# A sliding-window copy made of DMAs alone: twelve staged batches for eleven, and direct copies issued as halves

## The chip, the cores and the metric

The kernel runs on one core of one Trainium2 chip. Nothing is computed: every byte is moved by the core's 16 DMA engines, which serve three DMA queues, one issued from SyncE (SP, queue q1 in the profile), one from ScalarE (ACT, queue q10) and one from GpSimd (POOL, queue q0, a queue whose transfers software prepares). The metric is the device time of one execution in microseconds, the median of several runs.

## The reference: what is computed

```python
batch, length, dim = (32, 4096, 256)     # x is float32
window_size, stride = 64, 32
n_windows = (length - window_size) // stride + 1        # 127
for i in range(n_windows):
    start = i * stride
    result[:, i] = x[:, start:start + window_size].copy()
```

Since the window is two strides long, it is easiest to think in blocks of 32 rows, 32 KB each. A batch has 128 blocks, and window w of a batch is block w followed by block w + 1, 64 KB in one piece. So the output is nearly twice the input: 32 x 127 windows of 64 KB, 266 MB, from 134 MB.

## The kernel before

There are two ways to make a batch, and the kernel uses both at once.

**Direct.** `Copier.windows` (lines 29 to 38) copies from HBM to HBM. One call takes 16 windows, a "sixteen", so that each of the 16 engines gets one window. With `half=None` the call copies whole windows, 64 KB for each engine, 1 MB in all; the profile shows a window as two packets of 32 KB. With `half=0` or `1` it copies only the first or second block of each of the 16 windows, 32 KB for each engine and 512 KB in all, so that a sixteen takes two calls. A direct byte passes the DMA engines once, and is read from HBM as often as it is written.

**Staged.** `Staging.load` and `Staging.store` (lines 86 to 111) bring a batch into one of six SBUF tiles, a block to each of the 128 partitions, and store that tile twice: once as the first halves of all windows (`half=0`) and once as the second halves (`half=1`). A staged byte passes the engines once on its way in and twice on its way out, but is read from HBM once. The packets have 16 KB. `Staging.run` (line 116) issues all this on ScalarE's queue in the order six loads, twelve stores, then the loads and stores of the second group; a load waits until its tile's earlier stores are done.

A whole-tile store writes 128 half windows where a batch has 127, so it spills one junk half window into the batch before and one into the batch after. The neighbours are direct batches, and the 15 windows next to a staged batch are therefore kept out of the sixteens. These are the "edges" (lines 166 to 168): 20 of them with 15 windows, and one with 4. GpSimd's queue copies them at the end, after waiting for the neighbour's stores (`st.wait_stored`, line 196).

**Which batches.** Before, `staged` (line 143) is 1, 4, 7, ..., 31, eleven batches; the other 21 are direct, with seven sixteens each, 147 in all, every direct batch having one staged neighbour. Batch 31 is shifted by one block so that its spill falls into batch 30, whose last windows are copied by `columns` (lines 40 to 47), which cuts windows into 4 KB pieces; the very last two windows are issued from SyncE after batch 31's stores (lines 202 and 203).

**The order on SyncE.** The loop of line 175 issues the sixteens. A hand-made account (`turns`, `share`, lines 170 to 187) chooses between whole and halves: three sixteens in four are halved while ScalarE's queue loads, and 15 in 100 while it stores, with all halves at the start and near the second group of loads. In all 92 sixteens go whole and 55 as halves.

**The release of the software queue.** The semaphore `near` is raised by the last but one sixteen. GpSimd waits for it on line 192 and then issues its edges, the order being that of the list. The kernel ends when SyncE has seen all the counts (line 206).

Of the kernel before, what the change touches and what calls it, by code (L numbers as in the profile page):

```python
# [125 lines left out]
@with_exitstack  # L126
def kernel(
    ctx: ExitStack,
    tc: tile.TileContext,
    x: bass.AP,  # L130
    window_size: bass.AP,
    stride: bass.AP,
    out: bass.AP,
):
    nc = tc.nc
    W, S = int(window_size), int(stride)
    B, L, D = x.shape
    n_win = (L - W) // S + 1
    assert out.shape == (B, n_win, W, D)
    c = Copier(x, out, B, L, D, W, S, n_win)  # L140


    staged = [*range(1, B, 3)]
    items = [(b, -1 if b == B - 1 else 0, c.nb) for b in staged]
    place = {b: g for g, (b, _, n) in enumerate(items) if n == c.nb}
    direct = [b for b in range(B) if b not in staged]
    pool = ctx.enter_context(tc.tile_pool(name="xb", bufs=1))
    st = Staging(c, tc, pool, x.dtype, items, 6)
    ring_d, ring_s, ring_r = nc.sync, nc.scalar, nc.gpsimd
    done = tc.alloc_semaphore("done")  # L150
    near = tc.alloc_semaphore("near")
    rest = tc.alloc_semaphore("rest")
    total = {done: 0, near: 0, rest: 0}

    def count(dma, sem):
        dma.then_inc(sem, 16)
        total[sem] += 16

    sixteens = []
    for b in direct:
        w = 15 if b - 1 in staged else 0
        sixteens += [(b, w + 16 * j) for j in range((c.nw - w) // 16)]
    singles = [(B - 1, c.nw - 1, 1)]
    edges = [(b, 0 if b - 1 in staged else 112, 15) for b in direct[:-1]]
    last = B - 2
    edges.append((last, 112, 4))

    first_loads, loads, stores = 6 * 17, 5 * 17, 6 * 34  # L170
    turns = share = 0
    with tc.tile_critical():  # L172
        st.run(ring_s)

        for i, (b, w) in enumerate(sixteens):
            sem = near if i == len(sixteens) - 2 else done
            second = turns - first_loads - stores
            loading = turns < first_loads or 0 <= second < loads
            share += 120 if turns < 16 or -8 <= second < 16 else 90 if loading else 18
            if share >= 120:  # L180
                share -= 120
                turns += 4
                count(c.windows(ring_d, b, w, 16, 0), done)
                count(c.windows(ring_d, b, w, 16, 1), sem)
            else:
                turns += 3
                count(c.windows(ring_d, b, w, 16), sem)
            if i == len(sixteens) // 2:
                for b, w, half in singles:
                    count(c.windows(ring_d, b, w, 1, half, 2048), done)  # L190

        ring_r.wait_ge(near, 16)
        for b, w, n in edges:
            for k in (b - 1, b + 1):
                if k in place and b != last:
                    st.wait_stored(ring_r, place[k])
            count(c.windows(ring_r, b, w, n), rest)


        count(c.columns(ring_r, last, 116, 9), rest)  # L200
        ring_r.drain()  # L201
        st.wait_stored(ring_d, place[B - 1])
        count(c.columns(ring_d, last, 125, 2), done)
        total[st.ended] = st.count[st.ended]
        for sem, n in total.items():
            ring_d.wait_ge(sem, n)
# [35 lines left out]
```

## Time and profile before

| what | value |
|---|---|
| device time, median of 3 runs | 754.17 us (752.58 to 754.21) |
| span of the profiled execution | 742.1 us |
| median less the span (launch and end around the span) | 12.1 us |
| bytes that the DMA engines moved | 313.26 MB |
| HBM bytes read, written | 220.95 MB, 267.09 MB |
| SyncE: 1 MB copies, 512 KB copies | 92, 110 |
| ScalarE: loads, stores of 4 MB | 10, 21 (and ten smaller pieces) |
| GpSimd: edges of 960 KB | 20 |
| POOL's long wait for `near` | 648.7 us |

The profile gives the span of the execution that it recorded, and no device time of its own for it; what lies around the span is taken from the median, which makes the profiled execution's time 742.1 + 12.1 = 754.2 us. Packets are what the profile counts as a DMA engine's unit of work. Besides the data packets there is a completion packet of 4 bytes for each engine and DMA, which raises the semaphore. A DMA share of 1.00 means that all 16 engines are busy the whole time; it can come out slightly over 1, since the recorded times of following packets overlap a little.

### The profile page before, as it was taken

The page shows a single profiled execution, that of the slowest core. Times are in us where ns is not written, and L with a number is a line of the kernel's source. Part 1 is how long each engine was busy: PE and PEld are TensorE (multiplying, and loading weights), DVE is VectorE, ACT ScalarE, POOL GpSimd, SP SyncE. Part 2 cuts the span into 40 slices and gives each one's busy share as a digit, 9 for nine tenths or more (in the row PEclk, how much of TensorE's full clock was granted, in tenths as well). Part 3 has the DMA queues.
Part 4 walks back from the last instruction along what each step waited for, and adds up shares of the span by engine and source line. Part 5 has one row for each costly group of instructions (what it writes and reads, how often), then busy time and mean ns, then how long its engine had stood idle before and what let it go on. Part 6 is the DMA issues. An engine that isn't in the chain of part 4 may idle for free.

```text
span 742.1 us, 323 instructions
## 1 busy us (share of the span) xinstructions
POOL 12.7 (2%) x26
## 2 busy tenths in 40 slices
POOL 0000000000000000000000000000000000050100
DMA  8999999999999999999999999999999999999996
GB/s 361 424 430 427 435 431 428 423 435 425 428 427 426 428 428 420 429 435 427 427 427 412 433 435 431 427 436 432 434 424 429 430 424 426 428 435 432 421 420 253
DMA packets 18290, 313.26 MB, mean 422 GB/s; under 512 B 4336, under 2 KB 4336, under 8 KB 4528
## 3 DMA queue, kind: packets, MB, share of 16 engines
q1 hardware_dynamic: 8016, 154.32, 48.8%
q10 hardware_dynamic: 9104, 138.41, 44.0%
q0 software_dynamic: 1168, 20.51, 6.6%
q14 instruction: 2, 0.02, 0.0%
HBM read 220.95 MB, written 267.09 MB: 658 GB/s over the span
## 4 chain that ended last, share of the span: by engine, by line
another core or an unknown queue 92%; POOL 2%; issue 0%; POOLq 0%; SPq 0%
POOL out_dram L34 2%; POOLq L201 0%; POOLq L237 0%; SPq L172 0%; POOLq L114 0%
## 5 line engine op out<-in xcount | busy, mean ns | idle before, releaser
L34 POOL DMA_DIRECT2D out_dram<-in_x_dram x21 | 12.0, 575 | 685.4 <-DMA out_dram<-in_x_dram 648.7
L44 POOL DMA_DIRECT2D out_dram<-in_x_dram x1 | 0.6, 581 | 0.0
L223 POOL MEMSET const-float32-0.0<- 128x1 f32 x1 | 0.1, 98 | 0.2 <-issue 0.2
L223 POOL MEMSET const-bfloat16-1.0<- 128x1 bf16 x1 | 0.1, 101 | 0.0
L223 POOL MEMSET const-float32-1.0<- 128x1 f32 x1 | 0.1, 98 | 0.0
L223 POOL MEMSET const-uint8-127<- 128x1 uint8 x1 | 0.1, 98 | 0.0
## 6 DMA issues: line engine op xcount, KB each, us to landing
out_dram<-in_x_dram SPq DMA_DIRECT2D x92, 1024.0 KB, 99.8
out_dram<-xb ACTq DMA_DIRECT2D x21, 4096.0 KB, 138.5
out_dram<-in_x_dram SPq DMA_DIRECT2D x110, 512.0 KB, 90.2
xb<-in_x_dram ACTq DMA_DIRECT2D x10, 4096.0 KB, 130.5
out_dram<-in_x_dram POOLq DMA_DIRECT2D x20, 960.0 KB, 37.9
xb<-in_x_dram ACTq DMA_DIRECT2D x4, 1024.0 KB, 15.7
out_dram<-xb ACTq DMA_DIRECT2D x2, 1024.0 KB, 110.5
out_dram<-xb ACTq DMA_DIRECT2D x4, 512.0 KB, 94.4
```

The costliest lines, as they stand in the source:

```text
L34: return q.dma_start(out=self.oap((b * self.nw + w0) * 2 + h, [[2 * blk, n], row]), in_=self.xap(b * self.nb + w0 + h, [[blk, n], row]), m ...
L44: return q.dma_start(out=self.oap((b * self.nw + w0) * 2, [[part, 16], [2 * self.blk, n], row]), in_=self.xap(b * self.nb + w0, [[part, 16 ...
L223: nc = _bacc.Bacc("TRN2", target_bir_lowering=False, num_devices=1)
```

## The change

- Twelve batches are staged: 1, 4, 7, 10, 13, 16, 18, 20, 22, 25, 28 and 31. The 20 others are direct and have seven sixteens each, 140 in all. Batches 17, 19 and 21 now have a staged neighbour on both sides, so their sixteens begin at window 7, and they have two edges, of 7 and of 8 windows.
- The account of turns is gone. Every sixteen is issued as two halves, but for every eighth (the fifth, the thirteenth and so on), which goes whole: 17 whole, 123 as halves.
- Eight of the 16 edges that have 15 windows are issued as two halves each and stand in the list after the first four edges. The edge of batch 30 has 11 windows instead of 4, a number worked out so that the windows of all unsplit edges add up to a multiple of 16; the `columns` copy on GpSimd shrinks from 9 windows to 2.
- `near` is raised by the last but two sixteen.

```diff
-    staged = [*range(1, B, 3)]
+    staged = [1, 4, 7, 10, 13, 16, 18, 20, 22, 25, 28, B - 1]
...
-    sixteens = []
+    sixteens, edges, split = [], [], []
+    last = B - 2
     for b in direct:
-        w = 15 if b - 1 in staged else 0
-        sixteens += [(b, w + 16 * j) for j in range((c.nw - w) // 16)]
+        first = (15 if b + 1 not in staged else 7) if b - 1 in staged else 0
+        sixteens += [(b, first + 16 * j) for j in range((c.nw - first) // 16)]
+        if b != last:
+            edges += [(b, w, n, None) for w, n in ((0, first), (first + 112, 15 - first)) if n]
+    for e in [e for e in edges if e[2] == 15][4:12]:
+        edges.remove(e)
+        split += [e[:3] + (half,) for half in (0, 1)]
     singles = [(B - 1, c.nw - 1, 1)]
-    edges = [(b, 0 if b - 1 in staged else 112, 15) for b in direct[:-1]]
-    last = B - 2
-    edges.append((last, 112, 4))
-
-    first_loads, loads, stores = 6 * 17, 5 * 17, 6 * 34
-    turns = share = 0
+    odd = -sum(n for _, _, n, _ in edges) % 16
+    edges = edges[:4] + split + edges[4:] + [(last, 112, odd, None)]
+    whole = 8
+
     with tc.tile_critical():
         st.run(ring_s)
 
         for i, (b, w) in enumerate(sixteens):
-            sem = near if i == len(sixteens) - 2 else done
...
-            if share >= 120:
-                share -= 120
-                turns += 4
-                count(c.windows(ring_d, b, w, 16, 0), done)
-                count(c.windows(ring_d, b, w, 16, 1), sem)
-            else:
-                turns += 3
-                count(c.windows(ring_d, b, w, 16), sem)
+            for half in (None,) if i % whole == whole // 2 else (0, 1):
+                dma = c.windows(ring_d, b, w, 16, half)
+                count(dma, near if i == len(sixteens) - 3 and half != 0 else done)
...
-        for b, w, n in edges:
+        for b, w, n, half in edges:
             for k in (b - 1, b + 1):
                 if k in place and b != last:
                     st.wait_stored(ring_r, place[k])
-            count(c.windows(ring_r, b, w, n), rest)
-
-
-        count(c.columns(ring_r, last, 116, 9), rest)
+            count(c.windows(ring_r, b, w, n, half), rest)
+
+
+        count(c.columns(ring_r, last, 112 + odd, 13 - odd), rest)
```

More of the change, by code (lines that the diff above doesn't have):

```diff
@@ L175 @@
         for i, (b, w) in enumerate(sixteens):
-            sem = near if i == len(sixteens) - 2 else done
-            second = turns - first_loads - stores
-            loading = turns < first_loads or 0 <= second < loads
-            share += 120 if turns < 16 or -8 <= second < 16 else 90 if loading else 18
-            if share >= 120:
-                share -= 120
-                turns += 4
-                count(c.windows(ring_d, b, w, 16, 0), done)
-                count(c.windows(ring_d, b, w, 16, 1), sem)
-            else:
-                turns += 3
-                count(c.windows(ring_d, b, w, 16), sem)
+            for half in (None,) if i % whole == whole // 2 else (0, 1):
+                dma = c.windows(ring_d, b, w, 16, half)
+                count(dma, near if i == len(sixteens) - 3 and half != 0 else done)
             if i == len(sixteens) // 2:
```

## The prediction

> **What bounds the kernel now.** I begin with the page's slices and its queue table, because no engine computes and the chain of waits can't see inside the queues.
>
> ```profile
> DMA  8999999999999999999999999999999999999996
> GB/s 361 424 430 427 435 431 428 423 435 425 428 427 426 428 428 420 429 435 427 427 427 412 433 435 431 427 436 432 434 424 429 430 424 426 428 435 432 421 420 253
> DMA packets 18290, 313.26 MB, mean 422 GB/s; under 512 B 4336, under 2 KB 4336, under 8 KB 4528
> ...
> q1 hardware_dynamic: 8016, 154.32, 48.8%
> q10 hardware_dynamic: 9104, 138.41, 44.0%
> q0 software_dynamic: 1168, 20.51, 6.6%
> ...
> HBM read 220.95 MB, written 267.09 MB: 658 GB/s over the span
> ```
>
> All 16 engines are busy in every slice but the first and last; the three queues' shares add up to 99.4%. Time is therefore bytes over the engines' rate, plus the ragged ends. Next I ask for windows cut where ScalarE's queue turns from loads to stores (130 and 507 us) and back (404 us), and for the two ends.
>
> ```profile
> core 0: us, POOL busy (x), PEclk, DMA share, GB/s
> ...
> 60.00:130.00 70.00, 0.00 (x0) 1.00 1.01 430
> 130.00:404.00 274.00, 0.00 (x0) 1.00 1.01 428
> 404.00:507.00 103.00, 0.00 (x0) 1.00 1.01 430
> 507.00:649.00 142.00, 0.00 (x0) 1.00 1.00 428
> ...
> 730.00:735.00 5.00, 0.00 (x0) 1.00 0.88 353
> 735.00:738.00 3.00, 0.00 (x0) 1.00 0.20 81
> ```
>
> The share is 1.00 in every inner stretch; in the store stretches, where most sixteens go whole, the rate is 2 GB/s lower. The queue table of the stretch from 130 to 404 us shows how an engine divides itself:
>
> ```profile
> q1 hardware_dynamic: 3263, 66.85, 57.4%
> q10 hardware_dynamic: 3270, 50.30, 43.2%
> ```
>
> The packet counts are equal: the queues take turns packet by packet, the 4-byte completion packet using up a turn like any other. Last, the chain in order of time, for GpSimd's part:
>
> ```profile
> 177.90 470.92 another core or an unknown queue
> ...
> 649.11 10.25 POOL out_dram L34 x18
> 659.36 36.49 another core or an unknown queue
> ...
> 696.14 1.72 POOL out_dram L34 x3
> ```
>
> GpSimd issues 18 edges once `near` comes, waits 36 us for ScalarE's stores, and issues the rest with some 45 us to go. The engines are full meanwhile, so that wait costs nothing.
>
> **Part 1, twelve staged for eleven.** A staged batch passes 3 x 128 blocks of 32 KB, 12.58 MB; a direct one 127 x 64 KB, 8.32 MB. One batch changes sides: q10 gains 12.58 MB, q1 and q0 together lose 8.32 MB. Prices come from the table: q10 took 44.0% of 742.1 us, 326.5 us, for 138.41 MB, 2.359 us per MB; q1 and q0 took 55.4%, 411.1 us, for 174.83 MB, 2.352 us per MB. So +29.7 - 19.6 = **+10.1 us**. The trace's packet records agree: 768 more packets of 16 KB at a mean of 617.8 ns, 254 fewer of 32 KB at 1223.3 ns, over 16 engines, +10.2 us. By bytes alone, 4.26 MB at 428 GB/s, it is +10.0 us. Nothing hides this, since no engine is idle for it to fill.
>
> **Part 2, halves.** DMAs go from 204 + 41 + 22 = 267 to 265 + 44 + 32 = 341 (SyncE: 17 whole, 246 halves, 2 others; ScalarE: one load and two stores more; GpSimd: 8 edges of 15, 16 halves, six of 7 or 8, the one of 11, the columns). Each DMA gives each engine a completion packet, 9 ns in the records: 74 x 9 ns = **+0.7 us**. Splitting changes no data packet, 32 KB either way.
>
> The Trainium skill, "DMA: Bandwidth & Descriptors", speaks against it: "Anatomy of one DMA" gives each DMA some 2.0 us of fixed cost, and "Rules for kernel authors" wants at least 1 MiB. Were those 74 fixed costs in series, an estimate from that page would be 148 us and a time near 902 us; the stretches of loads, where three sixteens in four are halves already, run at 430 GB/s, not under the 428 of the others, so here they overlap.
>
> What halves may give back is the time that packets take above their least. The records' least for 32 KB is 1213 ns and for 16 KB 611 ns; all excess together is 7.6 us per engine. In the store stretches the 81 whole sixteens have a mean excess of 13.4 ns per packet (median of sixteens 7.5), the 16 halved ones a median of 0.5 but, with one burst of 147 ns at 401 us, a mean of 13.2. By the medians' row nearly all of the whole ones' 81 x 32 x 13.4 ns / 16 = 2.2 us goes, and up to 1 us on q10 beside them; by the means nothing. The stretches of loads have little excess though q10's traffic differs there too, so halves aren't proven to be the cause. I take **-1.5 us**, ends -4 and +1 (the burst's kind repeating: one such sixteen costs 32 x 147 / 16 = 0.3 us).
>
> **Part 3, turns and the release.** q1 had 92 x 3 + 55 x 4 = 496 turns and gets 17 x 3 + 123 x 4 = 543; q10 had 33 x 17 = 561 and gets 36 x 17 = 612. The rest of q10 when q1 ends goes from 65 turns to 69. GpSimd's list goes from about 70 turns to about 73 (a 15-window edge 3, two halves 4, an edge of 7 or 8 about 2). Both still end together, and one queue alone fills the engines (649 to 653 us shows q10 with hardly anything beside it at full rate). By bytes, `near` falls after 535 turns: 144.6 MB of q1 and 132 MB of q10, at 428 GB/s near 649 us, as now. Raising it one sixteen earlier covers the few us between POOL's wake and its first packet, which q10 fills already: 0. GpSimd's in-order waits: the edges of batches 27 and 29 wait for batch 28's stores, q10's turn 578, some 43 turns after `near`; 62 turns of GpSimd's work are issued ahead of them, so its queue isn't empty then. Behind that wait are four DMAs, 11 turns, against 39 left on q10: 0.
>
> **Part 4, the end.** Engines run out between 734.1 and 739.7 us, and the last two rows above show the loss: a mean of some 4.5 us per engine before the last packet. Edges are dealt to the engines in a ring; 304 windows before, 176 whole ones and 240 half ones after, are all multiples of 16, so both versions deal evenly and what differs is drift. The 4 KB pieces of `columns` shrink from 9 windows to 2 on GpSimd, -0.02 us. I take 0, ends -3 and +3.
>
> **Sum.** 10.1 + 0.7 - 1.5 + 0 = +9.3 us on 742.1 + 12.1 = 754.2, the profiled execution with what lies around it, which is the median: **763.5 us**, +1.2%.
>
> **The rivals.**
> (a) Nothing comes back: the halves save nothing and the end is longer by some us of drift. 754.2 + 10.8, and up to 3 for the end: 765 to 768. For it: the means of whole and halved excess are equal. Against: the medians.
> (b) HBM is the bound, and the change turns faster. A staged batch reads 4.19 MB of HBM where a direct one reads 8.32: HBM bytes fall from 488.0 to 484.0 MB, -0.83%, -6.2 us: 748. It decides if packets wait for HBM rather than for their engine. For it: the store stretches' 2 GB/s, and excess that strikes all engines in the same few us. Against: 84% of q1's 32 KB packets lie within 7 ns of the least time, which a shared memory would spread. The Trainium skill, "HBM Reference", Specifications, has 716 GB/s for a domain, and the page's 658 is near it; a bound by that ceiling would give the same 748 at best.
> (c) The bytes cost what I say, but nearly all excess goes (7.6 us) and part of the ragged end: 754.2 + 10.8 - 7.6 and up to -4, so 753 to 757, little or no change. For it: from 420 to 540 us the records show hardly any excess (0.02 us per engine), so it can vanish, and with whole sixteens too. Against: it comes back at 550 us, and 1.4 us of it falls after 700 us, where GpSimd's queue runs, which remains.
> (d) The change doesn't do what it says: an even dealing that fails would leave one engine with a window too many, 2 x 1.2 us, inside the end's bounds.
>
> **How the numbers follow.** Forecast 763.5 (own range 760.5 to 766): 0.65. (a) beyond that: 0.21, (c) 0.10, (b) 0.04. The range 758.5 to 767.5 takes in the forecast, most of (a) and the upper edge of (c), and joins the bounds of halves and end without adding all extremes. A measurement of this kernel can tell 0.3%, 2.3 us, from no change: faster 0.03, same 0.07 (most of (c)), slower 0.90.
>
> **What would show it.** Right: q10 at 151.0 MB, q1 at 147.0, q0 at 19.5, together 317.5 MB; some 5500 packets under 512 B; a DMA share still 1.00, and 428 to 431 GB/s in the middle; a span near 751; q1 and q10 near 52 and 48% of the store stretches; POOL's first edge near 649 us. Part 2 is wrong if the store stretches stay at 428 GB/s or fall; part 4 if the last packets spread over more than 9 us; part 1, and with it the sign, if the mean GB/s rises by over 1%, which is rival (b).

## The result, and the profile after

| | device time, median | ratio to before (95% interval) |
|---|---|---|
| before, 22 runs | 753.5 us (751.95 to 756.14) | |
| changed, 22 runs | 755.51 us (752.78 to 757.58) | 1.0025 (1.0015 to 1.0035) |

The change makes the kernel slower by 0.25%, some 2 us, where +9.3 us was forecast. The sign holds; the time lies under the range of 758.5 to 767.5.

The page of the changed kernel: slices, packets, queues (packets, MB, share of 16 engines' time) and HBM bytes.

```profile
DMA  8999999999999999999999999999999999999996
GB/s 357 412 430 427 417 433 431 432 432 431 431 430 431 430 431 431 430 429 431 420 418 419 432 430 430 430 431 424 433 430 431 430 432 435 432 423 425 432 379 256
DMA packets 19970, 317.53 MB, mean 421 GB/s; under 512 B 5600, under 2 KB 5600, under 8 KB 5680
...
q10 hardware_dynamic: 9920, 151.00, 47.4%
q1 hardware_dynamic: 8768, 146.98, 45.7%
q0 software_dynamic: 1280, 19.53, 6.2%
...
HBM read 216.83 MB, written 267.16 MB: 642 GB/s over the span
```

The bytes are those forecast, to the first decimal, and the engines are still full in every slice between the ends. Against the profile of before the rates hardly move: in the two stretches of stores they are 429 and 431 GB/s, where it had 428. Windows at the same borders (columns: stretch, length, POOL busy, granted clock, DMA share, GB/s), and below them the two hardware queues from 130 to 404 us:

```profile
60.00:130.00 70.00, 0.00 (x0) 1.00 1.00 425
130.00:404.00 274.00, 0.00 (x0) 1.00 1.01 429
404.00:507.00 103.00, 0.00 (x0) 1.00 1.00 429
507.00:649.00 142.00, 0.00 (x0) 1.00 1.01 431
```

```profile
q1 hardware_dynamic: 3641, 61.32, 52.5%
q10 hardware_dynamic: 3642, 56.23, 48.2%
```

The packets alternate as before, and SyncE's part of the bytes has fallen from 57% to 52%. GpSimd's first edge is issued at 653 us and its wait for ScalarE's stores ends at 710, with the engines full:

```profile
653.03 8.45 POOL out_dram L34 x16
...
670.47 39.51 another core or an unknown queue
...
710.26 1.73 POOL out_dram L34 x3
```

One line upsets the sum's footing. The span of this execution is 753.7 us and its own device time 755.5; in all 22 executions of the changed kernel the time is about 1.8 us over the span, and so it is in the 66 executions of before that are timed below. So what lies around the span is 1.8 us, not the 12.1 that I took for launch and end. By this the first profile of before, with a span of 742.1, was an execution of some 743.9 us (an estimate, 742.1 + 1.8): 10 us shorter than the median of its kernel, and 5 us under the fastest of its timed executions, 749.3. From that profile to this one the span grows by 11.6 us, from median to median the time by 2.

### The profile page after: what moved, and what is told of

Read it like the earlier page. It is cut to its first block, busy times and chain, and to the rows that moved or that the text cites. A ratio compares the mean times of both kernels' runs of the same rounds, so it can differ in the third digit from the quotient of the medians.

```text
span 753.7 us, 403 instructions
## 1 busy us (share of the span) xinstructions
POOL 17.6 (2%) x36
## 3 DMA queue, kind: packets, MB, share of 16 engines
q10 hardware_dynamic: 9920, 151.00, 47.4%
q1 hardware_dynamic: 8768, 146.98, 45.7%
q0 software_dynamic: 1280, 19.53, 6.2%
## 4 chain that ended last, share of the span: by engine, by line
another core or an unknown queue 92%; POOL 2%; issue 0%; POOLq 0%; SPq 0%
POOL out_dram L34 2%; POOLq L196 0%; POOLq L232 0%; SPq L176 0%; POOLq L114 0%
## 5 line engine op out<-in xcount | busy, mean ns | idle before, releaser
L34 POOL DMA_DIRECT2D out_dram<-in_x_dram x31 | 16.9, 552 | 694.7 <-DMA out_dram<-in_x_dram 652.6
L44 POOL DMA_DIRECT2D out_dram<-in_x_dram x1 | 0.5, 517 | 0.0
```

What stands on the lines that cost most here:

```text
L34: return q.dma_start(out=self.oap((b * self.nw + w0) * 2 + h, [[2 * blk, n], row]), in_=self.xap(b * self.nb + w0 + h, [[blk, n], row]), m ...
L44: return q.dma_start(out=self.oap((b * self.nw + w0) * 2, [[part, 16], [2 * self.blk, n], row]), in_=self.xap(b * self.nb + w0, [[part, 16 ...
```

## The experiments

Three theories came first. Theory 1: an ordinary execution of before loses 8 to 9 us in its whole sixteens, and halves don't lose it. Theory 2: halves do nothing, and the twelfth staged batch pays for itself in HBM bytes. Theory 3: the earlier release and the split edges shorten the end. Each run is set against before on the same chip, where before's median was between 751.0 and 754.2 us, so that it is the ratios that can be compared from run to run.

**A second profile of before (no edit).**

> The kernel before, unchanged, for a second profile. The timed executions of the changed kernel are all 1.8 us over their spans, so the first profile of before (span 742.1) would be an execution of 743.9 us, some 10 us under the median of its kernel. Theory 1 (halves): an ordinary execution of before has a span near 751.7 and packets that take some 17 us per engine above their least in all, not 7.6, most of it in the store stretches where sixteens go whole. Theory 2 (HBM bytes): the same span, but the excess lies as much in the load stretches. If the span is 742 again while the time is 753, the profiled and the timed executions differ in what lies around the span and both theories lose their ground.

751.41 us against 751.0 for before (ratio 1.0009, 0.9996 to 1.0022), span 751.0. Its windows and queues:

```profile
130.00:404.00 274.00, 0.00 (x0) 1.00 1.00 422
404.00:507.00 103.00, 0.00 (x0) 1.00 1.01 427
507.00:649.00 142.00, 0.00 (x0) 1.00 1.00 422
```

```profile
q1 hardware_dynamic: 3215, 66.23, 57.5%
q10 hardware_dynamic: 3212, 49.48, 42.9%
```

The first profile had 428 GB/s in these store stretches; the ordinary execution has 422, at the same 57% for SyncE. In the packet records the time above the packets' least (1213 ns for 32 KB, 611 ns for 16 KB) is 16.9 us per engine, where the first profile had 7.6 and the changed kernel has 7.8. Span and excess are those of theory 1. Most of the difference lies in the store stretches: 5.7 us between 130 and 390 us and 3.2 between 507 and 649, against 2.4 and 1.1 in the first profile and 1.3 and 0.3 in the changed kernel.

**Eleven staged batches, all else of the change kept.**

```diff
-    staged = [1, 4, 7, 10, 13, 16, 18, 20, 22, 25, 28, B - 1]
+    staged = [*range(1, B, 3)]
```

> The changed kernel with eleven staged batches again (1, 4, ..., 31); halves, split edges and the earlier release stay. Theory 1 (a staged batch costs its 4.3 MB, 10 to 11 us, and halves save 8 to 9 us): 755.5 - 10.5 = 745, faster than before by 1.1%. Theory 2 (the staged batch pays for itself by fewer HBM bytes, halves do nothing): 754 to 755, as before. Theory 3 (the release and the split edges shorten the end by several us): between, 748 to 752, with a shorter ragged end.

756.95 us, ratio 1.0075 (1.0058 to 1.0092): slower than before and, by the ratios, than the changed kernel (1.0025), against all three theories.

**Before with every sixteen halved.**

```diff
-            share += 120 if turns < 16 or -8 <= second < 16 else 90 if loading else 18
+            share += 120
```

> The kernel before with its account of turns fixed to halves, all 147 sixteens as two calls; eleven staged batches, old edges and old release. Theory 1: 745 to 746, faster by 1.0 to 1.2%, unless SyncE's queue, at 588 turns against 561 on ScalarE's, now ends so late that the edges run alone at the end; even then the engines stay full. Theory 2: 754 to 755. Theory 3: 754.

760.41 us, ratio 1.0120 (1.0101 to 1.0139). Both kernels lose their time in the same place. The page's slices and the windows of the first of them (eleven batches, halves):

```profile
GB/s 360 410 425 439 431 427 428 426 433 431 433 429 431 434 434 430 431 432 435 420 421 427 432 427 431 430 432 429 436 429 431 433 432 430 436 418 344 333 328 199
```

```profile
130.00:404.00 274.00, 0.00 (x0) 1.00 1.01 430
507.00:649.00 142.00, 0.00 (x0) 1.00 1.01 432
700.00:720.00 20.00, 0.00 (x0) 1.00 1.00 331
```

Up to 650 us halves do what theory 1 says: 430 to 432 GB/s in the store stretches. Then the rate falls to 331 with the engines busy all the while. With halves a sixteen takes four turns of SyncE's queue in place of three, and ScalarE's queue gets 48% of the bytes in place of 43%. So in the first kernel's packet records it ran dry at 686 us, SyncE's sixteens at 692, and the direct edges of GpSimd's queue were left alone until 752. Direct copies alone run at 331 GB/s: their packets take longer, so the DMA share shows 1.00 and hides it.

**Twelve staged batches, every sixteen whole.**

```diff
-    whole = 8
+    whole = 1
```

> The changed kernel with every sixteen whole (whole = 1); twelve staged batches, edges and release stay. Theory 1: the halves' saving is lost, 755.5 + 9 = 764, slower than before by 1.4%. Theory 2: 755, as the changed kernel. Theory 3: 755 too, with the same end.

775.5 us, ratio 1.0317 (1.0297 to 1.0338). By the ratios that is 2.9%, some 22 us, over the changed kernel, more than twice theory 1's price.

```profile
130.00:404.00 274.00, 0.00 (x0) 1.00 1.00 416
507.00:600.00 93.00, 0.00 (x0) 1.00 1.00 414
660.00:700.00 40.00, 4.46 (x8) 1.00 1.01 431
```

```profile
q1 hardware_dynamic: 3083, 66.62, 58.7%
q10 hardware_dynamic: 3085, 47.45, 41.8%
```

With SyncE at 58% of the bytes the rate is 416; from 660 us on, with SyncE's queue empty and only 7% of the bytes direct, it is 431. These four runs suggested theory 4. A direct byte is read and written in HBM and counts twice there, a staged byte once, so HBM traffic is the rate times (1 + direct share). From the tables above, 130 to 404 us: before again 422 x 1.572 = 664 GB/s, twelve whole 416 x 1.584 = 659; direct copies alone 331 x 2 = 662. With halves it is 429 x 1.522 = 653, and there the rate stops at some 430. Two ceilings, then: some 660 GB/s of HBM traffic and some 431 GB/s through the engines. That direct copies are merely slow by themselves doesn't fit, since staged packets wait too: between 130 and 390 us a 16 KB packet of ScalarE's queue takes a mean of 21.2 ns over its least with all sixteens whole, 11.9 in before again and 3.0 in the changed kernel. Whether the memory itself or the way to it sets the 660, no run separates. The rival, theory 5, is that whole sixteens collide as such.

**Whole sixteens at the share of halves.** Two turns with next to no bytes after every second sixteen.

```diff
-    whole = 8
+    whole = 1
...
+            if i % 2:
+                count(ring_d.dma_start(out=tiny[:, 16 * (i // 2) : 16 * (i // 2) + 16], in_=c.xap(b * c.nb + w, [[c.blk, 16], [1, 16]])), done)
```

> All sixteens whole, twelve staged, and after every second sixteen SyncE loads 16 x 64 bytes into a spare tile: two turns of its queue with next to no bytes, so that two whole sixteens and one such load take 8 turns for 128 KB per engine, as halves do. Theory 4 (two ceilings: the engines pass at most some 431 GB/s, HBM at most 650 to 665 GB/s, where a direct byte counts twice and a staged one once, and halves only lower SyncE's share of the bytes): the direct share falls from 58.5% to about 52%, the rate in the store stretches rises from 416 to 429 to 431 GB/s, and the time falls from 775.5 to 755 to 757, that of the changed kernel. Theory 5 (whole sixteens as such collide, halves as such don't): the rate stays near 416 and the time at 770 to 776.

757.27 us, ratio 1.0053 (1.0034 to 1.0071): by the ratios 2.6 of the 2.9% come back with no sixteen halved.

```profile
130.00:404.00 274.00, 0.00 (x0) 1.00 1.01 429
507.00:600.00 93.00, 0.00 (x0) 1.00 1.01 431
```

```profile
q1 hardware_dynamic: 3707, 60.20, 51.6%
q10 hardware_dynamic: 3708, 57.25, 49.0%
```

Theory 5 falls. It is SyncE's share, here 60.20 of 117.45 MB or 51%, that sets the rate, not the size of its copies.

**Direct copies by themselves.** The staging, the edges and the last columns are taken out; the loop issues

```diff
+            for half in (None,) if i < 70 else (0, 1):
+                count(c.windows(ring_d, b, w, 16, half), done)
```

> Direct sixteens alone on SyncE's queue, no staged batch and no edge (that output is left out): the first 70 whole, the other 70 as halves; 146.8 MB. Theory 4: both parts run at the HBM ceiling, 655 / 2 = 328 to 332 GB/s, whole or halved, engines shown as busy throughout, packets far over 1213 ns; the span is some 146.8 MB / 0.33 = 445 us and a few more. Theory 5: the halves run clearly faster, toward 400 GB/s, the whole ones slower. If the engines alone were the limit, both would run at 430 GB/s and the span would be 345 us.

The span is 451.4 us for 146.8 MB, in a single run; whole sixteens run in the first stretch, halves in the second:

```profile
100.00:200.00 100.00, 0.00 (x0) 1.00 1.00 330
300.00:400.00 100.00, 0.00 (x0) 1.00 1.00 328
```

That is 660 and 656 GB/s of HBM traffic, whole or halved.

**The rest of the change undone.** Twelve batches and halves stay; no edge is split, and the release is one sixteen later.

```diff
-    for e in [e for e in edges if e[2] == 15][4:12]:
+    for e in [e for e in edges if e[2] == 15][4:4]:
...
-                count(dma, near if i == len(sixteens) - 3 and half != 0 else done)
+                count(dma, near if i == len(sixteens) - 2 and half != 0 else done)
```

> The changed kernel with none of its edges split and the software queue released one sixteen later, as before; twelve staged batches and halves stay. Theory 4: within 1 us of the changed kernel, 755 to 756, since neither moves bytes; the end may differ by 1 to 2 us. A theory that the ends carry the result: over 2 us away from the changed kernel.

754.35 us, ratio 1.0010 (0.9995 to 1.0025), while the changed kernel has 1.0025 (1.0015 to 1.0035) and 1.0035 (1.0022 to 1.0047) in its two comparisons. Split edges and the earlier release gain nothing; whether they cost some 1 us, these intervals don't quite settle.

**Eleven batches with halves, edges spread over the run.** The first sixteen already releases GpSimd's queue, so that each edge goes as soon as its neighbours' stores are done.

```diff
-    staged = [1, 4, 7, 10, 13, 16, 18, 20, 22, 25, 28, B - 1]
+    staged = [*range(1, B, 3)]
...
-                count(dma, near if i == len(sixteens) - 3 and half != 0 else done)
+                count(dma, near if i == 0 and half != 0 else done)
```

> Eleven staged batches with halves, as in e1, but the software queue is released by the first sixteen, so that each edge goes as soon as its neighbours' stores are done and the direct edges are spread over the run in place of standing alone at its end. Theory 4: the 62 us in which direct copies ran alone at 331 GB/s go, the store stretches turn to three queues with a direct share near 57 to 60% at the HBM ceiling (about 415 to 420 GB/s), and by 488 MB of HBM traffic at 660 GB/s the time comes to 749 to 752, 5 to 8 us under e1, equal to before within 2 us. Theory 5: the store stretches stay at 430 GB/s, as they do with halves, and the time is 744 to 746.

758.98 us, ratio 1.0077 (1.0052 to 1.0102). The rate came as theory 4 had it, 420 GB/s in both store stretches with a direct share of (54.96 + 9.83) / 115.19 = 56%, 656 GB/s of HBM traffic; theory 5's 430 did not come. The time missed by 7 us. The edges come in bursts of a few, most of them 45 to 48 us apart, when a batch's stores end. Three bursts, each with the stretch behind it, and the queues of 130 to 404 us (an edge's packets start some 4 us after its issue, so that an issue is counted at the end of the stretch before):

```profile
176.00:189.00 13.00, 0.00 (x0) 1.00 0.99 392
189.00:223.00 34.00, 1.15 (x2) 1.00 1.01 430
223.00:236.00 13.00, 0.00 (x0) 1.00 1.01 396
236.00:271.00 35.00, 2.06 (x4) 1.00 1.01 428
271.00:286.00 15.00, 0.00 (x0) 1.00 1.01 397
286.00:317.00 31.00, 1.98 (x4) 1.00 1.00 423
...
q1 hardware_dynamic: 3267, 54.96, 47.8%
q10 hardware_dynamic: 3268, 50.40, 43.8%
q0 software_dynamic: 576, 9.83, 9.0%
```

So the two ceilings take turns: 392 to 397 GB/s while edges run, 423 to 430 between them. The even spread that the estimate took for granted did not come; that the bursts account for all of the 7 us isn't shown.

**Longer packets at an even share.** The packet records price a packet at 9 ns beyond its bytes (2 x 611 less 1213 ns; the expectations below have half of that, by a slip of mine), so I doubled all packets, keeping the share near 53%. As in the run with the rest of the change undone, no edge is split and the release is one sixteen later; the cut shows the rest:

```diff
-DIRECT, IN, OUT = 32768, 16384, 16384
+DIRECT, IN, OUT = 65536, 32768, 32768
...
-    whole = 8
+    whole = 1
```

> Twelve staged batches, unsplit edges, the release one sixteen before the end, every sixteen whole, and all packets twice as long: a window is one packet of 64 KB, a staged block one of 32 KB. SyncE's queue then gets 64 KB in 2 turns and ScalarE's 256 KB in 9, a direct share of 53%, nearly that of halves (52%) with half the packets. Theory 4 (two ceilings, shares by turns): the stretches stay at 428 to 432 GB/s, no return to the 416 of whole sixteens; the packet records price a packet at 4 to 5 ns and a completion packet at 9, so some 7100 packets and 123 DMAs fewer save 2 to 3 us: 751 to 753, level with before or just under it. Theory 5 (whole sixteens collide): 770 or more. If longer packets make the queues' ends more ragged, 754 to 757.

763.27 us, ratio 1.0163 (1.0141 to 1.0185). The store stretches are as forecast, with whole sixteens once more at the engines' rate; the second loads (423 GB/s from 404 to 507 us) and both ends are worse.

```profile
5.00:60.00 55.00, 0.00 (x0) 1.00 1.00 400
130.00:404.00 274.00, 0.00 (x0) 1.00 1.00 429
...
720.00:740.00 20.00, 0.00 (x0) 1.00 0.91 354
740.00:765.00 25.00, 0.00 (x0) 1.00 0.46 192
```

**The changed kernel once more, beside it.**

> The changed kernel unchanged, beside e8 and before on one chip. Both theories: 0.1 to 0.4% over before. The packet records should again show a direct share of 52% and 430 GB/s in the store stretches, and before's 57 to 58% at some 422.

754.07 us, ratio 1.0035 (1.0022 to 1.0047), as expected, with 430 and 431 GB/s in the two store stretches and 6.1 us of packet time above the least.

**Long packets only in the middle.** This one is built from the run with the rest of the change undone. Loads of the second group, the stores of the first ten batches and the sixteens from the 26th on are long; the edit passes the piece size to `load`, `store` and `windows`.

```diff
+            for half in (0, 1) if i < 25 else (None,):
+                dma = c.windows(ring_d, b, w, 16, half, 2 * DIRECT)
```

> e6 (twelve staged batches, unsplit edges) with long packets only where nothing begins or ends: the first 25 sixteens stay halves of 32 KB beside the first loads of 16 KB, then whole sixteens go as 64 KB packets beside loads and stores of 32 KB, and the last two batches' stores and the edges keep their short packets. Theory 4: the middle stays at 429 to 433 GB/s, the ends are those of e6, and some 5200 packets at 4.5 ns and 115 DMAs at 9 ns fewer per 16 engines save 2.5 us of e6: ratio to before 0.997 to 1.000, a version level with before or just faster. If long packets cost at every change between loads and stores, ratio 1.003 to 1.010.

756.41 us, ratio 1.0027 (1.0013 to 1.0041), where 0.997 to 1.000 was expected. The ends are mended (426 GB/s from 5 to 60 us), but the middle gives the saving back: 425 GB/s from 130 to 404 us and 423 from 404 to 507, against 430 and 428 in the kernel that it was built from. The 423 is that of the other kernel with long packets. Why, at a direct share of 52 to 53%, stays open. No version that I ran beats before.

## Why the prediction was right or wrong

**What bounds the kernel: half right.** The engines are full throughout, but a full engine isn't an engine at its own rate. Before's store stretches stood at the HBM ceiling; the changed kernel's stand at the engines'. The share of busy time, 1.00 in both, cannot tell them apart. GB/s times (1 + direct share) can.

**Part 1, the twelfth batch: right.** q10 has 151.00 MB, q1 146.98, q0 19.53, as forecast. At the packets' least times the work per engine rises from 727.0 to 737.1 us, +10.1 us.

**Part 2, completion packets: right.** Packets under 512 B rise from 4336 to 5600, their time per engine from 2.45 to 3.15 us, +0.7. The Trainium skill's fixed cost for each DMA ("DMA: Bandwidth & Descriptors", "Anatomy of one DMA", which is written for GpSimd's path, taken by 10 of the 74) does not show as time in series: the whole change costs 2 us, and the one term of the 74 DMAs that the records show is their completion packets.

**Part 2, the halves: the step that failed.** I took -1.5 us with ends of -4 and +1, since all the excess that I could see was 7.6 us. The ordinary execution has 16.9, and the changed kernel 7.8 and 6.1: -9.1 and -10.8 us, beyond the -4 that I allowed. It is the halves that do it and not the twelfth batch: with eleven batches and halves the excess up to 649 us is 3.8 us, where the ordinary before has 13.9. Two mistakes stand behind the number. I sized it in one execution without asking whether that execution was an ordinary one; the 12.1 us that seemed to lie around the span were the sign that it wasn't. And I looked for the cause in the shape of a whole copy, where it was the queue's share of turns: a whole window takes 64 KB in three turns, a half 32 KB in two, so halving cuts SyncE's bytes per turn from 21 to 16 KB. My part 3 counted exactly these turns, for the ends of the queues alone, and put them at 0.

**Part 3, the queues' ends.** GpSimd's first edge came at 653 us, forecast near 649, and its in-order waits cost nothing. But the sentence that one queue alone fills the engines was read from q10 and holds for staged bytes alone: direct bytes alone run at 326 to 331 GB/s. The changed kernel keeps q10 beside q0 to the end; eleven batches with halves don't, and lose there what halves won. That is what the twelfth batch does here: it pays 10.1 us of engine time to keep a staged queue running beside the direct ones.

**Part 4, the end.** Idle time per engine after 700 us, from the records, is 3.7 us in the second profile of before and 4.9 and 4.2 in the two of the changed kernel: +0.5 to +1.2, inside the ends I gave.

**The sum as it should have stood**, from the second profile of before to the two of the changed kernel: 10.1 + 0.7 - 9.1 + 1.2 = +2.9 against a measured +2.7 in the spans (751.0 to 753.7), and 10.1 + 0.7 - 10.8 + 0.5 = +0.5 against +0.3 (to 751.3). These add up what three single executions show. Single executions scatter by some 5 us, and these three were not all on one chip; the medians, each beside its own of before, rise by 2.0 and 2.5 us.

**The rivals.** (a) did not come: the excess fell by 9 to 11 us. (b), HBM as the bound, had the mechanism for before and the wrong consequence: with HBM relieved the engines bind at once. Its 748 came from scaling the time with the bytes and doesn't follow from a ceiling of 716 GB/s, which the 658 of the span did not reach. I dismissed it because 84% of q1's packets lay within 7 ns of the least; in the ordinary execution 71% do, and much of the loss is in the rest. (c) comes nearest to the size, little or no change by excess that vanishes, though 6 to 8 us of excess remain and nothing came off the ragged end.

What stays open is why the first profiled execution of before was 10 us shorter. In its store stretches it moved 428 x 1.571 = 672 GB/s of HBM traffic, where the second profile has 664. So the 660 is what the other executions show and not a limit that none can pass. A difference between chips is not ruled out.

## What to carry to other kernels

When DMA engines are busy throughout, work out the traffic of the memory behind them as well, with each byte counted as often as it crosses it; a copy within HBM counts twice, and the mix of queues at each moment decides which ceiling binds. Queues here share an engine packet by packet, so changing a copy's packets per completion changes every queue's share, and with it who is left alone at the end. Before taking a size from one profile, hold that execution's span against the median: a gap too large for a launch means that the execution isn't typical.

## What the runs showed of the hardware

- Copies within HBM, alone on the 16 engines, run at 326 to 331 GB/s, whole or halved, with the engines shown as fully busy; traffic that is nearly all staged (7% direct) runs at 431.
- The HBM traffic of this one core stands at 652 to 664 GB/s in reads and writes together, in stretches of 70 us and more where 56% or more of the bytes are direct; the first profile of before has 672. The Trainium skill, "HBM Reference", Specifications, gives 716 GB/s for a domain; over any 70 us the packet records reach 679 at most, in that first profile, and 669 in all others.
- The queues take turns at one profile packet each: 3641 to 3642, 3707 to 3708, and with three queues 3267 to 3268. The Trainium skill, "DMA: Bandwidth & Descriptors", "Queues, rings and completion order", says that the queues alternate packet by packet, which agrees, but expects some 9 to 17 descriptors in one; here a turn is a single packet of 16 to 64 KB, and the 4-byte completion packet takes a full turn.
- The commonest time of a packet is 2418 ns for 64 KB, 1213 for 32 KB and 611 for 16 KB: so a packet costs 8 to 9 ns beyond its bytes, as the completion packet does.
